# Norm weights as scales of the transposed copies instead of a spread row, and 24 identity transposes on TensorE before the first tile

## The chip, the cores and the metric

The kernel runs on one core of one Trainium2 chip. The metric is the device time of one execution in microseconds (us); lower is better.

## What is computed

One encoder layer is applied with the same weights to two requests: a prompt of 512 tokens and a sample of 1024 tokens, each 1024 wide, all in float32. Cut to what matters here:

```
h    = x * rsqrt(mean(x*x) + 1e-6) * g            # RMSNorm, g = norm_g (1024 weights)
proj = h @ w_in                                   # q, k, v of two attentions, gates z_a, z_b, g_a, g_b
oa   = neighbourhood attention(A) * silu(z_a);  ob = windowed attention with 8 heads on 2 k/v heads (B) * silu(z_b)
y    = x + (sigmoid(g_a) * (oa @ w_o_a) + sigmoid(g_b) * (ob @ w_o_b)) @ w_out
```

The norm weights g belong to the 1024 columns of x. The change concerns only the place where they are multiplied in for the prompt.

## The kernel before

**Precision.** Products are made of rounded parts: every operand v is kept as a high part (v rounded to the type fp32r) and a low part (v minus its high part), and each product is three matmuls, high by high, high by low, low by high. The parts of h are the tiles `hh` and `hl`, those of a weight piece `whi` and `wlo`. ScalarE (ACT) makes the high part with a copy, VectorE (DVE) or GpSimd (POOL) the low part with a subtraction.

**The order of the work.** The whole program is written as a list of operations with a priority, a guessed duration per engine and the operations that come before each (class `Flow`). A planner goes through them in a simulated time and lets each engine take the ready operation of the lowest priority number; where DVE and POOL can both do one, it picks the engine. What comes out is one fixed order of instructions per engine; on the chip the engines wait for each other by semaphores. So guessed durations set the order on every queue, also far behind the place where they stand. Operations that may run on either DVE or POOL, and those marked `port`, aren't planned on DVE and POOL at the same time. The piece `wlo` of the first weights is tied to POOL alone (`FIRST_POOL`), and an operation with one engine has no such mark unless it is given.

**The start.** The prompt is taken in four tiles t of 128 tokens. For each tile (`norm_tile`), with priority `NORM[t]` = -20, -1, 0, 1:

- SP's queue loads x into `xt`, 128 tokens on partitions by 1024 columns; ACT squares it and sums the squares (L460); POOL makes 1/rms per token, `nr`, in two steps (L464, L468).
- DVE multiplies `xt` in place by `nr` (one number per partition) and by the norm weights (L520), which here lie along the columns and so are needed as a row on all 128 partitions.
- TensorE (PE) transposes 128x128 pieces (L532) into PSUM, ACT copies them to `hh` (L537) and DVE subtracts to `hl` (L542): two pieces k at a time for tile 0, four at a time for tiles 1 to 3.
- Then the projection of the tile for the first attention group follows: 24 matmuls of 384 columns (L761), three for each of the eight pieces k of the contraction.

**The spread row.** The weights come twice from memory: as `gx` (128 partitions by 8, L1618), used much later for the sample, and as a row `norm_row` of 1024 numbers into the first partition of the tile `gb` (L1621; its tile is called `rb`). Four matmuls with a stationary row of ones (`one`) spread that row over 128 partitions into two PSUM banks (L1629, two records each). For tile 0, DVE reads the weights from those banks; ACT then copies the banks into `gb` (L1641), from which tiles 1 to 3 read them.

**`wake`** can issue pairs of transposes of the identity matrix into a PSUM bank that nobody reads. With `WAKE = 0` it issues none. The identity is made by POOL at the start.

The lines of the first group of weights (L600 loads, L602 `whi`, L607 `wlo`) run beside the first tiles. The first group's third and fourth piece lie in a tile that is called `bias` in the profile. The projections of the first group for four tiles, q and k (transposes L861, copies L882 and L896, subtractions L887 and L901), the attention, and later the large products of the gates and the output (L1284 to L1286) follow. L1010 and L1008 multiply attention weights by one number per partition, on DVE and POOL.

## Time and profile before

| | us |
|---|---|
| median of 3 runs (lowest, highest) | 1154.29 (1154.1, 1159.04) |
| time of the profiled execution | 1153.98 |
| its span, first to last instruction | 1152.2 |
| PE busy in the span | 1136.3 |
| DVE, ACT, POOL busy | 846.0, 663.3, 300.1 |

The profile is of one execution. Its time lies 0.3 us under the median of the runs shown, and its span 1.8 us under its own time. Busy is what the instruction records cover; the records of neighbouring instructions on one engine may overlap, so that the distance from start to start is shorter than the length of one record.

### The profile page before, as it was taken

Reading aid. Unit: us, or ns where it says so; the run is one execution under the profiler, and the core shown is the slowest. Engines: PE = TensorE matmul, PEld = TensorE weight load, DVE = VectorE, ACT = ScalarE, POOL = GpSimd, SP = SyncE. Lnnn points to the kernel's source line nnn. Section 1 sums busy time; section 2 is a strip of 40 time slices with the busy share of each in tenths; the row PEclk is TensorE's granted clock in tenths of the full one; section 3 lists DMA queues with packets and bytes.
Section 4 is the critical chain, followed back from the end, with each engine's and each line's share of the span. In section 5 each row is a group of like instructions: output and inputs, shape, how many; then the busy total and the mean of one; then the engine's idle time right before and its main releaser. Section 6 shows DMA issues by size and latency. Waiting matters only on the chain.

```text
span 1152.2 us, 18508 instructions
## 1 busy us (share of the span) xinstructions
PE 1136.3 (99%) x6139; PEld 984.3 (85%) x6139; DVE 846.0 (73%) x1963; ACT 663.3 (58%) x1489; POOL 300.1 (26%) x403
## 2 busy tenths in 40 slices
PE   8999999999999999999999999999999999999998
PEld 7899888888888899999998888888888888788887
DVE  6887777587775478887777788865887655497984
ACT  6777997554343357666679899955534334243320
POOL 4753433000020054353333324410121210032110
PEclk9999999999999999999999999999999999999999
DMA  7754534478786522121221113227666334574062
GB/s 267 258 160 143 171 95 119 119 240 260 244 274 209 164 71 67 24 73 34 65 67 48 49 29 83 71 59 250 197 167 199 111 110 158 198 230 127 28 223 87
DMA packets 124705, 159.86 MB, mean 139 GB/s; under 512 B 28297, under 2 KB 66961, under 8 KB 124610
## 3 DMA queue, kind: packets, MB, share of 16 engines
q1 hardware_dynamic: 124610, 158.69, 45.1%
q8 instruction: 48, 0.79, 0.3%
q14 instruction: 47, 0.39, 0.1%
HBM read 121.93 MB, written 41.44 MB: 142 GB/s over the span
## 4 chain that ended last, share of the span: by engine, by line
PE 88%; ACT 5%; DMA 3%; DVE 2%; issue 1%; POOL 1%; SPq 0%; ACTq 0%; POOLq 0%; DVEq 0%
PE p L761 21%; PE x L1285 9%; PE x L1286 9%; PE x L1284 9%; PE x L1063 5%; PE x L1026 4%; PE p L1284 4%; PE p L1285 4%; PE p L1286 4%; PE x L934 4%; PE d L1284 4%; PE d L1286 4%; PE d L1285 4%; ACT hb L662 2%; PE x L861 1%
## 5 line engine op out<-in xcount | busy, mean ns | idle before, releaser
L761 PE MATMUL p<-wlo,hh 128*128 128x384 f32 x384 | 133.3, 347 | 0.0
L761 PE MATMUL p<-whi,hh 128*128 128x384 f32 x384 | 133.0, 347 | 0.0
L761 PE MATMUL p<-whi,hl 128*128 128x384 f32 x384 | 131.8, 343 | 0.0
L978 ACT ACTIVATE sb<-sb,mx 128x384 f32<-128x384 f32 (+1 forms) x192 | 108.1, 568 | 16.5 <-DVE mx L969 16.3
L1167 ACT ACTIVATE whi<-raw 128x512 fp32r<-128x512 f32 (+1 forms) x140 | 81.3, 591 | 55.4 <-PE x L1285 32.2
L761 PE MATMUL p<-whi,hb 128*128 128x384 f32 x384 | 108.6, 347 | 1.6 <-ACT hb L662 1.5
L1037 DVE TENSOR_TENSOR pp<-x,pp 128x512 fp32r<-128x512 f32 (+1 forms) x136 | 83.1, 639 | 32.7 <-ACT pp L1032 31.9
L1285 PE MATMUL x<-hl,whi 128*128 128x512 f32 x264 | 102.7, 389 | 0.0
L1284 PE MATMUL x<-hh,whi 128*128 128x512 f32 x264 | 102.7, 389 | 0.0
L1286 PE MATMUL x<-hh,wlo 128*128 128x512 f32 x264 | 102.7, 389 | 0.0
L1172 DVE TENSOR_TENSOR wlo<-raw,whi 128x512 fp32r<-128x512 f32 (+1 forms) x113 | 72.0, 647 | 31.7 <-ACT whi L1167 31.7
L1284 PE MATMUL x<-T,whi 128*128 128x512 f32 x224 | 87.2, 390 | 1.5 <-ACT T L1167 1.5
L1285 PE MATMUL x<-T,whi 128*128 128x512 f32 x224 | 87.3, 390 | 0.2 <-DVE T L1172 0.2
L1286 PE MATMUL x<-T,wlo 128*128 128x512 f32 x224 | 87.1, 389 | 0.0
L1032 ACT ACTIVATE pp<-x 128x512 fp32r<-128x512 f32 (+1 forms) x136 | 72.1, 563 | 20.5 <-PE x L1026 19.7
L799 POOL TENSOR_TENSOR rs_r<-rs_v,mhalf 128x4 f32<-128x4 f32 (+1 forms) x72 | 80.5, 1119 | 5.3
L1172 POOL TENSOR_TENSOR wlo<-raw,whi 128x512 fp32r<-128x512 f32 x27 | 39.0, 1449 | 160.0 <-ACT whi L1167 113.7
L1063 PE MATMUL x<-pp,v 128*128 128x256 f32 (+1 forms) x368 | 78.8, 326 | 1.2 <-DVE pp L1037 1.2
L761 PEld LDWEIGHTS p<-whi,hb 128*128 128x128 f32 x384 | 69.2, 188 | 5.9 <-ACT hb L662 2.7
L761 PEld LDWEIGHTS p<-wlo,hh 128*128 128x128 f32 x384 | 72.8, 190 | 1.2 <-issue 0.5
L761 PEld LDWEIGHTS p<-whi,hl 128*128 128x128 f32 x384 | 72.7, 189 | 1.1 <-issue 1.0
L761 PEld LDWEIGHTS p<-whi,hh 128*128 128x128 f32 x384 | 72.7, 190 | 0.7 <-issue 0.5
(352 smaller groups left out, 2954.0 us busy)
## 6 DMA issues: line engine op xcount, KB each, us to landing
raw<-in_w_g_dram SPq DMA_DIRECT2D x76, 256.0 KB, 3.2
w<-in_w_att_dram SPq DMA_DIRECT2D x46, 384.0 KB, 3.5
ot<-o_d SPq DMA_DIRECT2D x36, 256.0 KB, 3.2
g_d<-C SPq DMA_DIRECT2D x34, 256.0 KB, 2.0
raw<-in_w_z_dram SPq DMA_DIRECT2D x32, 256.0 KB, 4.0
raw<-in_w_out_dram SPq DMA_DIRECT2D x32, 256.0 KB, 3.0
C<-g_d SPq DMA_DIRECT2D x24, 256.0 KB, 4.0
out_dram<-C SPq DMA_DIRECT2D x23, 256.0 KB, 2.0
```

Of the source, the lines that this page charges most:

```text
L761: pe.matmul(ps.t[:, :GW], part[u](k), mv.t[:, c], start=k == 0 and m == 0, stop=k == KC - 1 and m == 2,)
L799: lambda e: nc.gpsimd.tensor_tensor(r.t[:, :nn], rv.t[:, :nn], mhalf[:, :nn], op=ALU.pow),
L934: pe.matmul(pss[2 * pair + i].t[:, :width], q.t[rows, u, at : at + P], kv[:, tiles[0] : tiles[-1] + 1 : step], start=n == 0, stop=n == 2,)
L978: act.activation(sb.t[:, :width], sb.t[:, :width], AF.Exp, bias=mx.t[:, i : i + 1], scale=-1.0, accum_out=sm.t[:, i : i + 1],)
L1032: lambda e, pt=pt, pp=pp, nn=nn: act.activation(pp.t[:, 0, :nn], pt.t[:, :nn], AF.Copy),
L1037: lambda e, pt=pt, pp=pp, nn=nn: dve.tensor_tensor(pp.t[:, 1, :nn], pt.t[:, :nn], pp.t[:, 0, :nn].bitcast(F32), op=ALU.subtract),
L1063: pe.matmul(out(), v.t[:, vs], mv(), start=first, stop=last)
L1167: (("act", ACT_(n)),), lambda e: act.activation(hi(), src(), AF.Copy), prio,
L1172: lambda e: engines[e].tensor_tensor(lo(), src(), hi().bitcast(F32), op=ALU.subtract), prio,
L1284: pe.matmul(out, hi.t[:, cs], mh(), start=first and k == 0, stop=False)
L1285: pe.matmul(out, hi.t[:, cs], ml(), start=False, stop=False)
L1286: pe.matmul(out, lo.t[:, cs], mh(), start=False, stop=last and k == len(ws) - 1)
```

## The change

`norm_row`, its load, the ones, the four spreading matmuls and ACT's two copies of their banks go. DVE multiplies `xt` by `nr` alone, with a `tensor_scalar` whose operands all lie in SBUF. After the transpose the columns of x lie on partitions, so the weight is one number per partition: ACT's copy to `hh` takes it as its scale, and DVE's subtraction becomes a `scalar_tensor_tensor` that multiplies the transposed piece by the same number and subtracts `hh`. Each works on one piece k of 128 columns, since every piece has its own column of `gx`; so there are eight copies and eight subtractions per tile instead of four (tile 0) or two (tiles 1 to 3). The load of `gx` moves to the place of the row's load, second in SP's queue. `WAKE` becomes 12: 24 transposes of the identity, with priority 2 and nothing that they wait for but the identity.

```diff
-WAKE = 0
+WAKE = 12
@@ encoder_kernel
-    one = cpool.tile([1, P], F32, tag="one", name="one")
-    dve.memset(one, 1.0)
@@ norm_tile
-            ps, made = gains_row[k0 // 4]
-            if t == 0: ... weights from the PSUM bank ps
-            else: ... weights from gb.t, "port": True
             m = f.op(
-                (("dve", DVE_(n) + 60),),
-                lambda e, cols=cols, gv=gv: dve.scalar_tensor_tensor(
-                    xt.t[:, cols], xt.t[:, cols], r.t, gv(), op0=ALU.mult, op1=ALU.mult
-                ),
-                prio, **kw,
+                (("dve", 68 + 0.68 * n),),
+                lambda e, cols=cols: dve.tensor_scalar(xt.t[:, cols], xt.t[:, cols], r.t, None, op0=ALU.mult),
+                prio, use=[r], hold=[xt], port=True,
             )
...
-            a = f.op(
-                (("act", ACT_(n, False)),), lambda e, ks=ks, pv=pv: act.activation(hh.t[:, ks, tok], pv(), AF.Copy),
-                prio, use=[ps], hold=[hh],
-            )
-            b = f.op(
-                (("dve", DVE_(n)),),
-                lambda e, ks=ks, pv=pv: dve.tensor_tensor(
-                    hl.t[:, ks, tok], pv(), hh.t[:, ks, tok].bitcast(F32), op=ALU.subtract
-                ),
-                prio, use=[ps], after=[a], hold=[hh, hl],
-            )
-            out += [a, b]
+            for k in range(k0, k0 + step):
+                pv, gain = lambda k=k, ps=ps, k0=k0: ps.t[:, (k - k0) * P : (k - k0 + 1) * P], gx[:, k : k + 1]
+                to = lambda v, k=k: v.t[:, k, t * P : (t + 1) * P]
+                a = f.op(
+                    (("act", 250),), lambda e, pv=pv, gain=gain, to=to: act.activation(to(hh), pv(), AF.Copy, scale=gain),
+                    prio, use=[ps, gx_v], hold=[hh],
+                )
+                b = f.op(
+                    (("dve", 260),),
+                    lambda e, pv=pv, gain=gain, to=to: dve.scalar_tensor_tensor(
+                        to(hl), pv(), gain, to(hh).bitcast(F32), op0=ALU.mult, op1=ALU.subtract
+                    ),
+                    prio, use=[ps], after=[a], hold=[hh, hl],
+                )
+                out += [a, b]
@@ the start
-    f.dma(lambda: nc.sync.dma_start(gx, norm_g), 4096, 1, into=[gx_v])
+    f.dma(lambda: nc.sync.dma_start(gx, norm_g), 4096, START[0] + 0.1, into=[gx_v])
     wake()
-    gb = f.value(rb_pool, [P, NT_S], F32, "rb", 1)
-    row = f.dma(lambda: nc.sync.dma_start(gb.t[:1], norm_row.unsqueeze(0)), 4096, START[0] + 0.1, new=[gb])
-    gains_row = ... four matmuls with `one` into two banks
     for t in range(gp.nb):
         h_ops["p"][t] = norm_tile(
-            norm_p, x_p, gb, gains_row, *h_p, t, ...
+            norm_p, x_p, *h_p, t, ...
         )
-        for i, (ps, users) in enumerate(gains_row if t == 0 else ()):
-            ... ACT copies the bank into gb
```

## Rows read from the trace of the kernel before

**Rows 1.** The page: busy time of each engine, and PE's granted clock in 40 slices.

```profile
PE 1136.3 (99%) x6139; PEld 984.3 (85%) x6139; DVE 846.0 (73%) x1963; ACT 663.3 (58%) x1489; POOL 300.1 (26%) x403
...
PEclk9999999999999999999999999999999999999999
```

**Rows 2.** PE's waits after 10 us, longest first: total, times, longest.

```profile
PE x L1284 <- ACT T L1167: 1.5, 1, 1.5
```

**Rows 3.** PE's timeline from 4 to 17 us: start, length, instruction, count.

```profile
4.58 3.75 PE L1629 MATMUL x<-rb,one 1*128 1x256 f32 x8 [4.58 <-DMA rb<-in_norm_row_dram]
8.26 2.36 PE L532 MATMUL x<-ident,xt 128*128 128x128 f32 x8
10.27 0.67 PE L761 MATMUL p<-whi,hh 128*128 128x384 f32 x1
10.74 0.52 PE L761 MATMUL p<-wlo,hh 128*128 128x384 f32 x1
11.06 0.52 PE L761 MATMUL p<-whi,hl 128*128 128x384 f32 x1
...
13.55 0.34 PE L761 MATMUL p<-wlo,hh 128*128 128x384 f32 x1
...
14.24 0.34 PE L761 MATMUL p<-whi,hl 128*128 128x384 f32 x1
14.42 0.60 PE L532 MATMUL x<-ident,xt 128*128 128x128 f32 x4
...
16.72 0.34 PE L761 MATMUL p<-whi,hl 128*128 128x384 f32 x1
```

**Rows 4.** Timeline of the first 9 us, POOL and DVE.

```profile
0.99 0.29 POOL masks.py:199 TENSOR_SCALAR_AFFINE_SELECT ident<-ident 128x128 f32<-128x128 f32 x1
...
5.87 0.57 POOL L468 TENSOR_TENSOR nr<-nv,mhalf 128x1 f32<-128x1 f32 x1
6.40 1.81 POOL L607 TENSOR_TENSOR wlo<-w,whi 128x768 fp32r<-128x768 f32 x1
6.85 0.87 DVE L520 SCALAR_TENSOR_TENSOR xt<-xt,nr,x 128x256 f32<-128x256 f32 x2 [5.85 <-PE x L1629]
7.64 1.39 DVE L607 TENSOR_TENSOR wlo<-w,whi 128x768 fp32r<-128x768 f32 x1
```

**Rows 5.** Groups by line and shape, first 36 us: busy us, mean ns of one.

```profile
L542 DVE TENSOR_TENSOR hl<-x,hh 128x512 fp32r<-128x512 f32 x6 | 4.1, 690 | 2.3 <-ACT hh L537 2.2
L537 ACT ACTIVATE hh<-x 128x512 fp32r<-128x512 f32 x6 | 3.6, 598 | 5.1 <-PE x L532 5.1
...
L607 DVE TENSOR_TENSOR wlo<-bias,whi 128x768 fp32r<-128x768 f32 x2 | 1.9, 948 | 0.0
...
L882 ACT ACTIVATE kt<-x,gcol 128x128 fp32r<-128x128 f32 x3 | 1.1, 371 | 1.3 <-PE x L861 1.1
...
L887 DVE SCALAR_TENSOR_TENSOR kt<-x,gcol,kt 128x128 fp32r<-128x128 f32 x3 | 1.0, 350 | 1.5 <-ACT qt L896 1.5
```

**Rows 6.** Timeline around 448 and 460 us, DVE and POOL.

```profile
448.30 0.75 DVE L1010 TENSOR_SCALAR sb<-sb,rs 128x384 f32<-128x384 f32 x2
...
460.82 1.11 DVE L1010 TENSOR_SCALAR sb<-sb,rs 128x384 f32<-128x384 f32 x2
...
460.00 1.71 POOL L695 TENSOR_TENSOR bias<-mask,raw 128x192 f32<-128x192 f32 x3 [0.77 <-DVE mx L969]
```

**Rows 7.** Instructions on tile `xt`: ns min/median/max, first to last start, forms.

```profile
L532 PE MATMUL x<-ident,xt x32: 271/273/476, 8.3 to 28.5; 128*128 128x128 f32 x32
```

**Rows 8.** ACT's timeline from 15 to 22 us; idle time before in brackets.

```profile
15.06 0.60 ACT L537 ACTIVATE hh<-x 128x512 fp32r<-128x512 f32 x1 [2.24 <-PE x L532]
...
21.15 0.37 ACT L882 ACTIVATE kt<-x,gcol 128x128 fp32r<-128x128 f32 x1 [1.15 <-PE x L861]
21.42 0.36 ACT L896 ACTIVATE qt<-x,gq 128x128 fp32r<-128x128 f32 x1
```

**Rows 9.** Timeline of SP's queue at the load of `gx`.

```profile
4.79 0.43 SPq L1618 DMA_DIRECT2D gx<-in_norm_g_dram  x1
```

More of the change, by code (lines that the diff above doesn't have):

```diff
@@ L362, in encoder_kernel @@
     norm_g: bass.AP,
-    norm_row: bass.AP,
     w_att: bass.AP,
@@ L503, in scaled_parts, with norm_tile @@
         return out
-    def norm_tile(pool, x, gb, gains_row, hh, hl, t, prio, load_prio, after=(), load_after=()):
+    def norm_tile(pool, x, hh, hl, t, prio, load_prio, after=(), load_after=()):
         xt, r = rstd(pool, x, t, prio, load_prio, 4, after, load_after)
-        tok = slice(t * P, (t + 1) * P)
         step, out = 2 if t == 0 else 4, []
         for k0 in range(0, KC, step):
-            n, cols, ks = step * P, slice(k0 * P, (k0 + step) * P), slice(k0, k0 + step)
-            ps, made = gains_row[k0 // 4]
-            if t == 0:
-                c = slice(k0 % 4 * P, k0 % 4 * P + n)
-                gv, kw = lambda ps=ps, c=c: ps.t[:, c], {"use": [r], "hold": [xt, ps], "after": [made[k0 % 4 // 2]]}
-            else:
-                gv, kw = lambda cols=cols: gb.t[:, cols], {"use": [r], "hold": [xt, gb], "after": made, "port": True}
-            m = f.op(
-                (("dve", DVE_(n) + 60),),
-                lambda e, cols=cols, gv=gv: dve.scalar_tensor_tensor(
-                    xt.t[:, cols], xt.t[:, cols], r.t, gv(), op0=ALU.mult, op1=ALU.mult
-                ),
-                prio, **kw,
-            )
-            if t == 0:
-                made.append(m)
+            n, cols = step * P, slice(k0 * P, (k0 + step) * P)
+            m = f.op(
+                (("dve", 68 + 0.68 * n),),
+                lambda e, cols=cols: dve.tensor_scalar(xt.t[:, cols], xt.t[:, cols], r.t, None, op0=ALU.mult),
+                prio, use=[r], hold=[xt], port=True,
+            )
             ps = bank("x")
@@ L1617, in encoder_kernel @@
     f.stage(-1000, open=(r_h, d0["p"], rb_pool, early["p"], late["p"], norm_p), make=h_p)
-    f.dma(lambda: nc.sync.dma_start(gx, norm_g), 4096, 1, into=[gx_v])
+    f.dma(lambda: nc.sync.dma_start(gx, norm_g), 4096, START[0] + 0.1, into=[gx_v])
     wake()
-    gb = f.value(rb_pool, [P, NT_S], F32, "rb", 1)
-    row = f.dma(lambda: nc.sync.dma_start(gb.t[:1], norm_row.unsqueeze(0)), 4096, START[0] + 0.1, new=[gb])
-    gains_row = []
-    for i in range(2):
-        ps, made = bank("x"), []
-        for j in range(2):
-            cols, out = slice(i * 512 + j * 256, i * 512 + j * 256 + 256), slice(j * 256, j * 256 + 256)
-            made.append(f.op(
-                (("pe", 850),),
-                lambda e, ps=ps, cols=cols, out=out: pe.matmul(ps.t[:, out], one, gb.t[:1, cols], start=True, stop=True),
-                NORM[0] - 1, hold=[gb], after=[row], **({"into": [ps]} if j else {"new": [ps]}),
-            ))
-        gains_row.append([ps, made])
     for t in range(gp.nb):
         h_ops["p"][t] = norm_tile(
-            norm_p, x_p, gb, gains_row, *h_p, t, NORM[t], START[t], h_ops["p"][t - GATE][::2] if t >= GATE else (),
+            norm_p, x_p, *h_p, t, NORM[t], START[t], h_ops["p"][t - GATE][::2] if t >= GATE else (),
             h_ops["p"][0][-1:] if t > 1 else (),
         )
-        for i, (ps, users) in enumerate(gains_row if t == 0 else ()):
-            gains_row[i][1] = [f.op(
-                (("act", ACT_(512, False)),),
-                lambda e, ps=ps, i=i: act.activation(gb.t[:, i * 512 : i * 512 + 512], ps.t, AF.Copy),
-                NORM[1] - 1, use=[ps], hold=[gb], after=users[2:],
-            )]
     setup(norm_p, -0.7, h_ops["p"][1][:1])
@@ L1728, in _layout @@
         "norm_g": inp["norm_g"][0].reshape(KC, P).T,
-        "norm_row": inp["norm_g"][0],
         "w_att": np.stack(groups),
```

1 line of the change is left out of this document (removed).

## The prediction

> **What bounds the kernel now.** I read the page first. PE is busy for 1136.3 of 1152.2 us and the granted clock is at its upper level, 2.4 GHz, in every slice [rows 1]. The list of PE's waits comes next: after 10 us the longest single one is 1.5 us [rows 2]. So from about 10 us on the kernel is one nearly unbroken stream of matmuls. Its end is the time at which that stream starts, plus the PE work, plus few small gaps. The change touches only the first 30 us, so I went on to PE's timeline there.
>
> PE first spreads the weight row, from 4.58 to 8.33 us; then it transposes tile 0; the first projection matmul starts at 10.27 us and the last of tile 0, the 24th, ends at 16.72 + 0.34 = 17.06 us [rows 3]. The distance from start to start is the thing to look at: 11.06 - 10.74 = 0.32 us early on, but (14.24 - 13.55) / 4 = 0.173 us later, for the same 384 columns [rows 3]. 384 columns in 0.32 us is 1.2 GHz. The slices of the page don't show this start, the pace does. Ten matmuls take 13.55 - 10.27 = 3.28 us, at the later pace 1.73: the low clock costs 1.55 us here. Before it rose PE had been at the spreading matmuls for 3.75 us (a stationary operand of one row), at eight transposes and at three microseconds of full matmuls.
>
> Then the timeline of the other engines, to see what tile 0 waits for. `nr` is ready at 5.87 + 0.57 = 6.44 us; DVE's first multiplication starts at 6.85 and is put down to PE's spread; a `wlo` of 1.39 us stands between DVE's second and third [rows 4].
>
> **The change, part by part.** The sum is made against the profiled execution's 1153.98 us, 0.3 us under the median of the runs.
>
> *The row goes.* Two waits end: DVE's for the spread (6.85 instead of about 6.5) and that of PE, which couldn't transpose before 8.26. DVE loses one memset in idle time, the PSUM banks of the row are free earlier. ACT's two copies of 128x512 go, about 0.6 each by the like-shaped copies [rows 5].
>
> *What DVE's multiplication meets instead.* It becomes an operation whose operands are all in SBUF. POOL starts its `wlo` of 1.81 us at 6.40, a moment before DVE could start, and holds on until 8.21 [rows 4]. Do the two get in each other's way? Three rows bear on it. The old multiplication with weights in PSUM took 0.87 for two beside this same POOL instruction. DVE's `wlo`, all in SBUF, started at 7.64 in its second half and took 1.39, where the same shape takes 0.948 elsewhere [rows 4, 5]: 0.44 longer, as if it stood until 8.08. And two `tensor_scalar` of 128x384 took 0.75 at one place and 1.11 beside POOL subtractions [rows 6]. I take it that DVE's first multiplication stands until 8.08. The other bound is a start at 6.5. The planner doesn't see this: `wlo` of the first piece is tied to POOL and carries no mark.
> The Trainium skill says the same more sharply (SBUF — State Buffer, section "SBUF: two separate sides"): DVE and GpSimd share one pair of ports, which goes as an exclusive lock for a whole instruction to whichever starts first, and a DVE operation wants it with two SBUF inputs or in a two-port mode. By that rule the multiplication stands until 8.21; without it the first projection would start some 1.6 us sooner.
>
> *From there to the first projection matmul.* One `tensor_scalar` of 128x384 costs 0.34 to 0.41 from the pair in 0.75 [rows 6], and 128x256 is no longer: 8.08 + 0.37 = 8.45. A transpose's record is 0.273 long in the middle of its group, and four took 0.60, so they start (0.60 - 0.273) / 3 = 0.11 apart at the high clock and, taken twice, 0.22 at the low one [rows 3, 7]. Two of them, with the length of the second and the hand-overs, end at 8.9 to 9.0. One copy with a scale per partition costs 0.371 [rows 5]: 9.3 to 9.4. I put the first matmul at 9.4, against 10.27.
>
> *Then the supply of the 24.* PE itself needs 24 x 0.173 = 4.15 us and two fours of tile 1's transposes at up to 0.60 [rows 3]: 9.4 + 4.15 + 1.2 = 14.75 at the high clock, 1.55 more, 16.3, at the low one. DVE from 8.08 has four multiplications (4 x 0.3 = 1.2), eight subtractions of 0.27 to 0.350 (the longer end is the row's record, the shorter is the distance that ACT's like pair shows, 21.42 - 21.15 [rows 5, 8]; 2.2 to 2.8), three `wlo` of 0.948 (2.85) and two multiplications of tile 1 (about 0.45 each): it ends at 15.2 to 15.8, and its last pieces may lie behind tile 0's end. I take 15.2 for the end of tile 0 against 17.06: 1.86 us.
>
> *The 24 transposes of the identity.* The identity is ready at 0.99 + 0.29 = 1.28 [rows 4]. At 0.22 us each they end at 1.4 + 24 x 0.22 = 6.7, ahead of the 8.45 at which PE is next wanted, so they cost nothing. At the pace of tile 0's eight with their pauses, 2.36 / 8 = 0.30 each [rows 3], they end at 8.6. Whether they raise the clock no row shows. The spread's one-row matmuls kept PE at work for 3.75 us and the clock stayed low after them; but these transposes fill 128 by 128, like the matmuls under which it rose. I take it that they raise it. DVE being the limit, this is worth not 1.55 but 16.3 - 15.2 = 1.1 at most.
>
> *Tiles 1 to 3.* ACT makes 24 copies, started every 0.27, instead of six of 0.598: 6.5 - 3.6 = 2.9 us more. Its idle time before two instructions of this stretch alone is 2.24 + 1.15 = 3.39 [rows 5, 8], and PE can begin on a single piece. DVE makes 24 subtractions (6.5 to 8.4) instead of six of 0.690 (4.1), and saves some 2 us on its six multiplications of 512 columns (two of 256 took 0.87 [rows 4], the new ones about 0.45). If ACT's idle time can't be used the 2.9 are PE's; I charge 0.1. Lower bound nothing, upper 2.9.
>
> *The load of `gx`.* It goes from the tenth place of SP's queue to the second; its issue of 0.43 us [rows 9] now stands ahead of the first weights and tile 1's x, in place of the row's issue, and leaves a gap in front of tiles 2 and 3. That is a shift of 0.1 to 0.2 for loads that nothing waits on by that much; nothing, up to 0.4.
>
> Sum: 1.86 - 0.1 = 1.8 us gained, 1153.98 - 1.8 = 1152.2. PE's stream behind it is the same and carries this to the end.
>
> **Rivals.**
>
> *The clock stays low.* Then tile 0 ends at 16.3 instead of 15.2, and the gain is 17.06 - 16.3 = 0.8, less 0.1: 1153.3. For it speaks that 3.75 us of PE work on the spread didn't raise the clock; against it that those were one row wide.
> The Trainium skill has this as a rule (TensorE: Matmul & The Clock Gate, section "PE-mode transpose"): the full clock doesn't engage for transposes, since they don't count as PE activity in the same way. No row here has transposes alone for long, so the trace neither bears it out nor refutes it.
>
> *DVE isn't held by POOL.* The chain starts 1.6 us sooner, first matmul at 7.8, DVE's supply ends at about 14; with POOL's `wlo` at 8.21 still wanted by the second matmul, tile 0 ends at 14.2 to 14.8. Gain 2.3 to 2.9: 1151.4.
>
> *The gain is given back.* ACT's idle gaps lie where it waits for transposes, so the 2.9 more may not fit into them; two thirds of it on PE's path eat the gain: 1154.0, within 1 us to either side.
>
> *Slower: the identity transposes hold PE.* If at the low clock they aren't pipelined, 24 records of the longest length, 0.476 [rows 7], end at 1.4 + 11.5 = 12.9 instead of 8.45; the first matmul is then at 13.8, tile 0 ends at 19.2, and the kernel takes 1156.2. It decides from (8.45 + 1.86 - 1.4) / 24 = 0.37 us each. Against it: eight transposes at the low clock took 2.36 us with pauses among them [rows 3].
>
> *The rest of the plan falls out differently.* New guesses and fewer operations shift every later decision between DVE and POOL. PE's idle time after 10 us is small, the longest piece 1.5 [rows 2], so little is to be won there: some 4 us more by a lucky order would bring 1148. A transfer that comes too late can cost more, with four or five waits of that size 1160.
>
> **Numbers.** Forecast 0.28; clock stays low 0.18; DVE not held 0.15; given back 0.12; PE held by the identity 0.05; another order 0.22 (0.10 ends over 0.5% faster, 0.07 over 0.5% slower, 0.05 between). 0.5% is 5.8 us, about what a measurement of this kernel tells from no change. Every case but the last two parts of another order lies inside that: 0.10 faster, 0.83 same, 0.07 slower. The forecast is 1152.2, its own range 1151 to 1153.5 from 15.8 and 14.75 for tile 0's end and the bounds of tiles 1 to 3 halfway. The range for 8 in 10 takes in the rivals up to the held PE and a part of the other orders: 1147.5 to 1156.2.
>
> **What would show it.** The first projection matmul starts near 9.4 and tile 0's last ends near 15.2. DVE's first `tensor_scalar` has a record of nearly 2 us or starts near 8.1; at 6.5 with 0.4 the port step is wrong. The first projection matmuls are 0.17 apart if the clock is up, 0.32 if not. Of PE's identity transposes the last ends before 7. ACT's idle brackets between 13 and 28 us shrink, and PE gets no new wait for `hh`. The prediction fails if PE's stream shows other gaps after 40 us than before: that would be the order, not the start.

## The result, and the profile after

The changed kernel takes 1157.91 us (median of 20 runs, 1156.18 to 1162.68) against 1154.34 us of before (20 runs, 1152.53 to 1159.04). The ratio is 1.0036 with a 95% interval of 1.0025 to 1.0046: slower, by less than the 0.5% that the prediction called no change, but outside its range of 1147.5 to 1156.2. The profiled execution took 1157.09 us, with a span of 1155.3. Three runs of the experiments that follow, one of f_order and two of f_dve0, took 1250 us or more and are left out of every figure.

The page of the changed kernel answers to [rows 1]. TensorE is as full as before; nothing here says where 3 us went.

```profile
PE 1140.2 (99%) x6155; PEld 986.1 (85%) x6155; DVE 844.8 (73%) x1971; ACT 664.8 (58%) x1507; POOL 303.2 (26%) x418
...
PEclk9999999999999999999999999999999999999999
```

PE's timeline of the first 18 us answers to [rows 3].

```profile
1.34 5.36 PE L442 MATMUL d<-ident 128*128 128x128 f32 x24 [1.34 <-POOL ident masks.py:199]
6.94 0.44 PE L518 MATMUL x<-ident,xt 128*128 128x128 f32 x2 [0.23 <-DVE xt L510]
8.76 0.96 PE L518 MATMUL x<-ident,xt 128*128 128x128 f32 x6 [1.37 <-DVE xt L510]
9.47 0.42 PE L749 MATMUL p<-whi,hh 128*128 128x384 f32 x1
9.73 0.34 PE L749 MATMUL p<-wlo,hh 128*128 128x384 f32 x1
10.41 0.69 PE L749 MATMUL p<-whi,hl 128*128 128x384 f32 x1 [0.34 <-DVE hl L530]
10.89 0.52 PE L749 MATMUL p<-whi,hh 128*128 128x384 f32 x1
11.21 0.52 PE L749 MATMUL p<-wlo,hh 128*128 128x384 f32 x1
...
15.52 0.34 PE L749 MATMUL p<-whi,hl 128*128 128x384 f32 x1
15.69 1.03 PE L518 MATMUL x<-ident,xt 128*128 128x128 f32 x8
17.78 0.44 PE L749 MATMUL p<-whi,hh 128*128 128x384 f32 x1 [1.06 <-ACT hh L525]
```

The identity transposes end at 6.70 and the first projection matmul starts at 9.47 (it was 10.27). What stood in between isn't quite what was forecast. VectorE's first scaling took 0.35 us, as GpSimd's `wlo` started only 0.12 us behind it; it was the second that stood (the two together read `6.53 2.17`). ScalarE had a new wait of 1.09 us for the second weights, so that its first copy came at 8.42. VectorE and GpSimd at the first scaling, then ScalarE:

```profile
6.53 0.35 DVE L510 TENSOR_SCALAR xt<-xt,nr 128x256 f32<-128x256 f32 x1 [5.67 <-POOL nr L465]
6.65 1.89 POOL L595 TENSOR_TENSOR wlo<-w,whi 128x768 fp32r<-128x768 f32 x1 [0.16 <-ACT whi L590]
```

```profile
7.67 0.84 ACT L590 ACTIVATE whi<-w 128x768 fp32r<-128x768 f32 x1 [1.09 <-DMA w<-in_w_att_dram]
```

On to the clock. The first two projection matmuls are 0.34 to 0.42 long, the next ones 0.52 and 0.32 apart: the clock was up and fell again. The windows of the same trace say when (start:end, length, busy time and count of each engine, granted clock, DMA share, GB/s); the clock is at 0.50, its lower level, from about 10 to 13.3.

```profile
6.50:10.00 3.50, 1.89 (x12) 1.08 (x10) 3.47 (x5) 2.20 (x8) 1.89 (x1) 1.00 0.99 382
10.00:13.30 3.30, 2.96 (x10) 2.89 (x10) 3.30 (x11) 3.30 (x8) 0.00 (x0) 0.50 1.02 406
13.30:17.00 3.70, 3.42 (x23) 3.15 (x21) 2.18 (x6) 1.20 (x4) 1.24 (x3) 0.99 0.70 228
```

Tile 0's 24th matmul ends at 15.86 in place of 17.06. But the eight transposes of tile 1, which before stood among the 24, now stand behind them and end at 15.69 + 1.03 = 16.72: for the same work the lead is 0.34 us. Then tile 1 loses it. PE waits 1.06 us for the copies, and ScalarE's timeline shows why: it squares tile 2 first, from 16.32 on, and makes the eight copies from 17.36. This is read from the trace; no run moved the square. TensorE's matmul at 17.78 follows the end of the first copy, 17.36 + 0.37, so it doesn't wait for the others.

```profile
16.32 1.06 ACT L457 ACTIVATE junk<-xt 128x1024 bf16<-128x1024 f32 x1
17.27 0.20 ACT L457 ACTIVATION_READ_ACCUMULATOR junk<-xt 128x1 f32 x1
17.36 2.17 ACT L525 ACTIVATE hh<-x,gx 128x128 fp32r<-128x128 f32 x8
```

PE's waits after 10 us answer to [rows 2]. The wait of 1.5 us of before is gone, others are there:

```profile
PE x L849 <- DVE qk L804: 1.3, 3, 0.8
PE p L749 <- ACT hh L525: 1.1, 1, 1.1
...
PE x L1272 <- ACT hh L1155: 0.9, 1, 0.9
```

To place them I laid the two streams of matmuls over each other: each matmul counts with its time at the full pace for its columns, and the table gives, for a moment of the profiled run of before, how much later (in us) the other kernel's profiled run had done as much work. It is my working from the traces, of all the kernels that follow too. Each row is one execution, which can lie off its kernel's median: f_wake38's took 1155.47 us (median 1158.18), b_wake's 1158.30 (1156.18), a_guess1's 1170.06 (1167.45).

```
time in before    12    19    27    37    62   163   310   365   431   527   970  1002
after           -0.5   1.6   1.3   1.6   1.4   1.9   2.5   4.1   3.5   4.6   4.5   3.2
a_nowake        -0.3   1.5   1.2   1.5   1.5   2.3   2.9   7.7   7.2   7.2   6.9   6.3
a_guess1        -0.1   4.0   3.8   4.5   4.4   9.6  10.0  17.0  16.6  18.1  17.9  16.0
a_ot3           -0.5   1.8   1.5   1.7   1.4   2.7   3.3   4.4   3.9   4.9   4.9   3.5
f_order          0.3  -0.1   1.6   1.8   2.1   2.4   2.4   2.4   2.4   2.4   2.3   2.1
f_wake38        -0.7  -1.0   0.6   0.8   1.1   0.9   0.9   0.9   1.2   2.2   2.0   1.2
f_gx5            0.2  -0.1   1.5   1.7   2.5   1.8   1.8   1.8   1.2   2.6   2.5   1.1
f_dve0          -0.4   0.6   2.2   2.4   2.3   1.7   1.7   2.1   1.5   1.5   1.4   0.8
f_nowake         0.3   0.5   2.1   2.3   2.7   2.3   2.3   2.3   1.9   1.9   1.9   0.6
f_fill          -0.7  -0.8   0.8   1.0   1.3   1.3   1.2   1.4   2.5   3.3   3.2   2.2
f_nosplit        1.1   2.1   1.9   1.5   2.8   2.6   2.7   2.7   2.0   3.3   3.1   2.4
f_fill_ns       -0.7  -1.3  -1.6  -2.0  -0.9  -1.4  -1.4   0.3   1.3   2.4   2.2   0.8
b_wake           1.7   1.2   1.2   1.2   2.4   3.2   3.2   3.2   4.5   5.5   5.2   4.3
b_guess1         0.4   0.5   0.3  -0.1   1.5   1.2   2.1   2.1   1.9   1.9   1.8   1.3
b_lag1950       -0.3  -1.0  -0.6  -0.6   0.5  -2.2  -2.2  -2.2  -3.3  -3.1  -4.6  -6.4
a_lag1950       -0.4   0.5   0.2  -0.1   2.0  -0.7  -0.7  -0.7  -1.7  -1.5  -2.8  -5.1
b_lag2950        0.2   0.6   3.5   3.4   3.0   1.7   3.5   3.5   2.5   2.2   2.1  -0.3
a_lag2950       -0.3   1.5   1.2   1.2   0.5  -0.6   0.4   0.4  -0.6  -0.9  -1.1  -3.4
```

The changed kernel is ahead at 12 us, 1.6 behind at 19, and 1.4 at 62: the start, the whole of what the change edits, costs 1.4, and it is lost between 16.7 and 19 us. Another 1.1 comes bit by bit from 62 to 310, and then it is single places: 1.6 at 361 (the wait of 0.9 for `hh` above, and what follows it), 1.1 at 523 (a wait of 0.8 for `qk`, the longest of the three above). Some 0.6 comes back before 431 and 1.3 near 985, where before had its wait of 1.5 us [rows 2] and this kernel has none.

No instruction out there was edited. But the planner writes out the order of all engines from guessed durations, and it made another order: of the 6131 matmuls that both traces have, the spread and the identity transposes apart, at least 324 stand at another place. So there are two theories: A, the order far behind the start costs the time; B, the change's own instructions cost it.

### The profile page after: what moved, and what is told of

Its sections match the earlier page's. It is cut to its first block, busy times and chain, and to the rows that moved or that the text cites. A ratio compares the mean times of both kernels' runs of the same rounds, so it can differ in the third digit from the quotient of the medians.

```text
span 1155.3 us, 18585 instructions
## 1 busy us (share of the span) xinstructions
PE 1140.2 (99%) x6155; PEld 986.1 (85%) x6155; DVE 844.8 (73%) x1971; ACT 664.8 (58%) x1507; POOL 303.2 (26%) x418
## 4 chain that ended last, share of the span: by engine, by line
PE 81%; ACT 7%; DMA 4%; DVE 4%; issue 2%; POOL 1%; SPq 0%; ACTq 0%; DVEq 0%; POOLq 0%
PE p L749 21%; PE x L1273 9%; PE x L1274 8%; PE x L1272 8%; PE x L1051 4%; PE x L1014 4%; PE x L922 4%; PE p L1273 4%; PE p L1272 4%; PE p L1274 4%; PE d L1272 3%; PE d L1273 3%; PE d L1274 3%; ACT hb L650 2%; PE x L849 1%
## 5 line engine op out<-in xcount | busy, mean ns | idle before, releaser
L966 ACT ACTIVATE sb<-sb,mx 128x384 f32<-128x384 f32 (+1 forms) x192 | 108.7, 573 | 17.2 <-DVE mx L957 16.9
```

Source lines behind the costliest of these rows:

```text
L966: act.activation(sb.t[:, :width], sb.t[:, :width], AF.Exp, bias=mx.t[:, i : i + 1], scale=-1.0, accum_out=sm.t[:, i : i + 1],)
```

## The experiments

Kernels f_ have the change's instructions in the order of before: the planner is given before's operations and durations, and only what they emit is the change's. One thing is not as in the change: an operation of before covers a whole bank, so a kernel f_ issues a bank's copies one after the other and its subtractions behind them, where the change plans each piece by itself. Kernels a_ are the change itself, b_ the kernel before, each with the edit shown. Each experiment had runs of before beside it, with medians of 1153.36 to 1153.85; all ratios are against those.

**The order and the instructions apart.**

```
f_order:  planner's operations and durations as before;
          what they emit as in the change (24 transposes where the row was spread)
b_guess1: -                (("dve", DVE_(n) + 60),),
          +                (("dve", 68 + 0.68 * n),),
a_nowake: -WAKE = 12
          +WAKE = 0
f_wake38: f_order with 38 identity transposes in place of 24
```

f_order: 

> The change's instructions (multiplication by 1/rms alone, copies and subtractions with the weight as scale, 24 identity transposes, early load of the weights, no spread row) in the order of the kernel before on every engine: the planner is given the operations of before with their guesses. Theory A, that the other order behind the start costs the time: as fast as before or faster, 1152 to 1154.5 us. Theory B, that the change's own instructions cost it (more ACT and DVE work, DVE held by POOL, a clock that falls back): 1157 to 1159 us, like the changed kernel.

b_guess1: 

> The kernel before with every instruction as it was; only the planner's guess for the multiplication at the start is the one of the change, 68 + 0.68 n instead of 128 + 1.04 n ns. That moves about as many instructions in the queues as the change did. Theory A: it is off from before by 1 us or more, in either direction, with a gap or two of PE that before doesn't have. Theory B: within 0.7 us of before, 1153.6 to 1155.

a_nowake: 

> The changed kernel without the 24 identity transposes; every other instruction stands in the same order on every engine. If the transposes raise the clock and it is lost again before the projections: within 0.5 us of the changed kernel, 1157.4 to 1158.4, with the projections 0.32 us apart until about 13.4 in both. If the transposes delay the start: faster by 0.5 to 1 us. If the high clock at the first pieces is worth something: slower by 0.3 to 0.6 us.

f_wake38: 

> As the run with the order of before, but 38 identity transposes instead of 24, which at the high clock last until about 8.2 us and so leave no pause of PE before the first tile's transposes. If the clock of the changed kernel fell because PE stood between 6.7 and 9.5 us, the projections start at the high clock and stay there, tile 0 ends up to 1.5 us sooner than with 24, and the time is 0.5 to 1.5 us below that run. If the transposes don't hold the clock up, 0.32 us apart from about 10 to 13.4 as with 24, and no difference.

Measured: f_order 1155.93 us, ratio 1.0022 (1.0013 to 1.0032); b_guess1 1154.53, 1.0006 (0.9997 to 1.0015); a_nowake 1159.28, 1.0047 (1.0035 to 1.0060); f_wake38 1158.18, 1.0040 (1.0025 to 1.0054). Neither theory is alone right. In the order of before the change still costs 2 us, between 19 and 37 us in the table, and has no stall at 361: between what A and B had forecast. One guess changed in before moves its stream by up to 2.1 us on the way, and its median hardly, as B had it. The identity transposes are worth nothing that the total shows: a_nowake lies at 1.0047, its interval overlapping the change's, and f_nowake, further down, takes what f_order takes. They do raise the clock; without them, in the same order, the first two projection matmuls are at the lower pace:

```profile
9.97 0.67 PE L749 MATMUL p<-whi,hh 128*128 128x384 f32 x1
10.44 0.52 PE L749 MATMUL p<-wlo,hh 128*128 128x384 f32 x1
```

But there the records are short from 13.00 on, in the change only from 13.43 on. In f_wake38, where TensorE stood for 0.63 us behind the identity transposes and not for 1.93 as in f_order, the clock stays up and the start is 1 us sooner. The windows of f_order and of f_wake38:

```profile
10.00:13.30 3.30, 3.30 (x13) 3.30 (x14) 2.97 (x10) 3.30 (x10) 0.68 (x2) 0.55 1.02 408
10.00:13.30 3.30, 3.15 (x19) 2.77 (x20) 3.30 (x11) 2.99 (x8) 0.51 (x1) 1.00 1.04 421
```

Its median is higher than f_order's all the same, where 0.5 to 1.5 us less was expected; its profiled run is its shortest and doesn't show why.

a_nowake's trace shows what a stall can draw after it. PE's waits of 355 to 372 us:

```profile
PE x L1272 <- ACT hh L1155: 2.3, 1, 2.3
```

and its windows behind that wait; the clock is at its lower level for 3.4 us, so that the stall cost it 4.8 us in all (2.9 to 7.7 in the table):

```profile
360.00:364.60 4.60, 2.09 (x9) 1.10 (x7) 3.21 (x7) 2.41 (x5) 1.28 (x1) 1.00 0.61 179
364.60:368.00 3.40, 3.40 (x8) 2.38 (x8) 2.50 (x4) 1.04 (x2) 0.00 (x0) 0.50 0.86 277
```

**The 2 us that stay in the order of before.** In f_order the first copies and subtractions of tile 2 read so, ScalarE's timeline and VectorE's:

```profile
22.89 1.14 ACT L535 ACTIVATE hh<-x,gx 128x128 fp32r<-128x128 f32 x4
```

```profile
24.06 1.12 DVE L540 SCALAR_TENSOR_TENSOR hl<-x,gx,hh 128x128 fp32r<-128x128 f32 x4 [0.94 <-ACT hh L535]
```

VectorE waits until all four copies of the bank are made, and then needs 1.12 us. Before it was one copy of 0.598 and one subtraction of 0.690 [rows 5]. In the changed kernel itself VectorE doesn't wait so: in tile 3 its first subtraction starts at 25.29, while the third copy lasts until 24.64 + 0.88 = 25.52, and in the table that kernel loses nothing between 19 and 62 us. So what f_order loses can't be carried over to the change as the cost of its pieces.

```profile
24.64 0.88 ACT L525 ACTIVATE hh<-x,gx 128x128 fp32r<-128x128 f32 x3 [0.49 <-PE x L518]
```

```profile
25.29 0.33 DVE L530 SCALAR_TENSOR_TENSOR hl<-x,gx,hh 128x128 fp32r<-128x128 f32 x1
```

Three edits to f_order take one suspect each; f_nosplit takes the pieces away:

```
f_nosplit: f_order, ScalarE's copy and VectorE's subtraction whole for each bank, no weights
f_gx5:     f_order, load of gx issued behind w0, w1 and xt of tile 1, not second
f_dve0:    f_order, +  e = "dve" if engs == ("pool",) else e      (the first wlo)
a_guess1:  the change, planned durations only: copy 250 -> 371, subtraction 260 -> 350
```

f_nosplit: 

> f_order (the change's instructions in the order of before) with the copies and subtractions whole again, as before: one ScalarE copy and one VectorE subtraction for each bank in place of four of each; the norm weights are left out of the prompt altogether, so the output lacks them there. Theory B1, that the 48 split pieces cost f_order its time (a bank's subtraction starts 1.14 us after its first copy in place of 0.60 and takes 1.13 in place of 0.69, for six banks behind tile 0): tiles 2 and 3 end about 1 us sooner than in f_order, and the time is 1153.5 to 1154.5, at most that of before. Theory B2, that the early load and the held VectorE cost it: the time stays at about 1156 (ratio to before 1.002).

f_gx5: 

> f_order with one edit: the 128-packet load of the norm weights is issued fifth on SyncE's queue, behind w0, w1, xt0 and xt1, instead of second. Theory B2 (the packets of 32 bytes keep the 16 DMA engines from the large loads in the first 6 us): ScalarE's second whi of w1 waits under 0.2 us where it waited about 1.1, the DMA rate of 3 to 6 us goes back from 354 to about 410 GB/s, and the time is 0.5 to 1 us lower than f_order's (about 1155.2). Theory B1 (the split pieces cost it): the start looks like that and the time stays at about 1156. If the load now comes too late for tile 0's first copy, that copy starts later than in f_order by the lateness.

f_dve0: 

> f_order with one edit: the first wlo subtraction, which GpSimd does from 6.6 to 8.1 us while VectorE's first scaling of tile 0 is held, is done by VectorE behind that scaling. Theory of the prediction (the scaling is held by GpSimd's work): the first scaling takes about 0.4 us in place of 2.1, tile 0's transposes end about 1 us sooner (8.8 in place of 9.8), and the first projection matmul comes at about 9.6 to 10 in place of 10.6; the time falls by at most that 1 us and, if the lead is lost again behind the start as in f_wake38, by nothing (1156). Rival: the scaling waits for its data; then it stays at 2 us and nothing moves.

a_guess1: 

> The change with every instruction as it is, and only the two planned durations by which its order is made put to what the trace shows for the split pieces (ScalarE's copy planned at 371 in place of 250 ns, VectorE's subtraction at 350 in place of 260). Theory A (the order far behind the start decides a few us): the progress of TensorE departs from the change's by 1 to 3 us at places far behind the start, such as the stall at 361, and the time differs from the change's by 1 us or more either way. Theory B (the change's own instructions): the time stays within 1 us of the change's 1157.9.

Measured: f_nosplit 1155.67, 1.0018 (1.0006 to 1.0031); f_gx5 1154.70, 1.0015 (1.0005 to 1.0025); f_dve0 1155.02, 1.0017 (1.0007 to 1.0027); a_guess1 1167.45, 1.0128 (1.0098 to 1.0159). The first three can't be told from f_order by their time, so what they say is read from the traces.

f_gx5: the DMA rate of 3 to 6 us is 408 GB/s, against 354 in f_order, 326 in the changed kernel and 410 in before, and ScalarE's wait of 1.0 for the second `w` is gone. Over all profiles it is less clear. With the load second in the queue (11 kernels) the rate is 322 to 370 and that wait 0.6 to 2.2 us; with it fifth (f_gx5, f_fill, f_fill_ns, f_fill_ot3) 374 to 408 and none to 0.3. But before and the four b_ kernels, without it at the start, have 348 to 410 and none to 0.8. So the load holds back the large ones, but single executions of before differ by nearly as much. At 12 us TensorE has 0.1 us of it.

f_dve0's first scaling shows that GpSimd had held it; in f_order its two took `6.51 2.15`:

```profile
6.44 0.35 DVE L518 TENSOR_SCALAR xt<-xt,nr 128x256 f32<-128x256 f32 x1 [5.58 <-POOL nr L466]
6.71 0.95 DVE L606 TENSOR_TENSOR wlo<-w,whi 128x768 fp32r<-128x768 f32 x1
```

The first projection matmul then comes at 9.90 in place of 10.61; the low clock lasts to 15.2 us, and the lead is used up.

f_nosplit has no wait of PE at all from 17 to 34 us, where f_order has 2.1, but its start is 0.8 us later (ScalarE waited 2.2 us for the second weights, and the second `wlo` is at 9.37 in place of 8.58) and its clock stays low until 16.8, which eats the 2 us: not decided by its time, which lies where the theory B2 had it.

a_guess1 is the large one: every instruction as in the change, two planned durations put to what the trace shows, and the time rises by 0.9%. Its table row loses at 19, between 62 and 163, and 7 us at 361. The order alone moves this kernel by 9.5 us. A good part of that goes through the clock. Where TensorE had stood (for 1.73 us until 163.73, for 2.33 until 372.49), it fell again:

```profile
163.70:167.10 3.40, 3.37 (x14) 3.33 (x15) 3.08 (x10) 2.38 (x6) 0.20 (x1) 0.50 0.24 67
371.90:378.70 6.80, 6.21 (x14) 4.67 (x15) 2.58 (x4) 1.68 (x3) 0.00 (x0) 0.50 0.67 229
```

With 10.1 to 16.9 us that is 17.0 us at the lower level against 3.4 in the changed kernel. The same matmul takes about twice as long there (0.32 against 0.173 from start to start), so my estimate is half of the 13.6 us between them, 6 to 7 of the 13.0 us between the two profiled runs.

**The start mended, and each half alone.**

```
b_wake:    before, -WAKE = 0   +WAKE = 12       (order of all the rest unchanged)
f_nowake:  f_order without the identity transposes
f_fill:    f_gx5 and f_dve0 together, and ahead of tile 0's later transposes
           +  for u in range(6 if t == 0 and k0 else 0):
           +      pe.transpose(ps.t[:, u % 2 * P : u % 2 * P + P], ident, ident)
f_fill_ns: f_fill with whole copies and subtractions, no weights
```

b_wake: 

> The kernel before with the 12 pairs of identity transposes alone; all other instructions and their order are those of before. Theory: the 24 transposes end at about 6.5 to 6.7 us, the rows of the spread matmuls behind them run at the higher clock (under 2 us in place of 3.4 us), and tile 0's transposes then wait for its squares and scaling as before. If the clock stays up, tile 0's last matmul ends 1 to 2 us sooner than 17.06; if it falls again at about 10 as in the change's trace, under 1 us. The total moves by at most that, 1152.5 to 1154 against 1153.5 of before; with the lead lost behind the start it is the same. The prediction's rival that identity transposes only hold TensorE would give up to 0.3 us more than before.

f_nowake: 

> f_order without the identity transposes: the norm weights as scales alone, in the order of before. Theory B1 (split copies and subtractions cost about 2 us in tiles 1 to 3, the head gives some of it back): first matmul at about 10 to 10.6 at the lower clock until about 13.4, tile 0 ends at 16.5 to 17, the gaps of 20 to 31 us stay at about 3.4 us in all against 1.05 in before, and the time is 1.5 to 2.5 us above before (1155 to 1156). Rival: the transposes themselves cost it; then it is at 1153.5 to 1154.5.

f_fill: 

> f_order with the load of the norm weights fifth on the queue, the first wlo subtraction on VectorE, and 6 more identity transposes ahead of each of tile 0's second, third and fourth group of transposes, so that TensorE hardly stands between 6.5 and 9.5 us. Theory (the granted clock fell to 0.50 for 3.4 us behind the first matmuls because TensorE had mostly stood between the identity transposes and them): the clock now stays at 1.0, tile 0's 24 projection products come 0.17 apart, and its last ends at 14 to 15 us in place of 17.06 of before. Then 2 to 2.5 us are lost to the split copies of tiles 1 to 3, and the time is 1153 to 1154.5, about that of before. Rival: the fall comes at fixed times and not from standing; then the low stretch stays.

f_fill_ns: 

> f_fill with whole copies and subtractions, one for each bank, as before; the norm weights are left out of the prompt, so the output lacks them there. Theory B1 (the split pieces lose about 2 us in tiles 1 to 3): the gaps of 17 to 32 us fall from about 3.4 us to about 1, the lead of tile 0 is kept, and the time is 1 to 2 us lower than f_fill's, below that of before (1151.5 to 1152.5). Theory A2 (any lead at the start is lost behind it at the weights and loads that pace the rest): the time is within 0.5 us of f_fill's though the gaps are gone.

Measured: b_wake 1156.18, 1.0024 (1.0011 to 1.0038); f_nowake 1155.52, 1.0018 (1.0005 to 1.0030); f_fill 1155.88, 1.0016 (1.0004 to 1.0028); f_fill_ns 1154.27, 1.0003 (0.9992 to 1.0014).

b_wake, which I had expected at or below before, starts its first projection matmul at 11.98 in place of 10.27: with the spread's matmuls still there the transposes hold TensorE, the last six of them among tile 0's own. Alone, the wake costs 1.2 us at the start. The 18 transposes ahead of the spread (4.10 us) didn't raise the clock here: the spread takes 3.78 us where it took 3.75, under 2 being expected, and the first projection matmuls are 0.32 apart.

f_fill keeps the clock up. Its windows, to be held against those of the changed kernel above (PE busy for 2.89 in place of 1.89 us, then 1.00 in place of 0.50):

```profile
6.50:10.00 3.50, 2.89 (x22) 2.42 (x23) 2.88 (x6) 2.19 (x5) 0.27 (x2) 1.00 1.02 379
10.00:13.30 3.30, 3.01 (x20) 2.69 (x19) 3.11 (x10) 3.17 (x9) 0.57 (x1) 1.00 1.03 417
```

So the clock had fallen behind TensorE's standing, which f_wake38 against f_order shows with that edit alone; no fixed time does it. Tile 0's 24 and two fours of transposes end at 15.91 + 0.34 = 16.25, not at the 14 to 15 expected: the first comes at 10.36 only, and two fours of transposes, a gap of 0.46 us with a wait for `wlo`, lie between. And f_fill loses 1.6 us between 19 and 27, f_fill_ns doesn't. PE's waits of 17 to 34 us in f_fill, where f_fill_ns has none:

```profile
PE x L867 <- DVE qk L822: 1.2, 2, 0.8
PE x L535 <- DVE xt L523: 0.9, 2, 0.7
```

That settles it for this order and for pieces issued bank by bank: they cost 2.1 us of waits in tiles 1 to 3. (The two intervals of the total overlap; the waits are what decides.) But f_fill_ns, 2.0 us ahead at 37, ends 0.8 behind: it loses 1.7 at 361, 1.0 at 400, 1.1 at 521, the same places where the changed kernel and others lose, each at some of them.

**What stands at those places.** f_gx5 and f_dve0 have the same order there, and one stalls at 521 and the other doesn't. VectorE's timeline in f_gx5:

```profile
520.81 1.59 DVE L698 TENSOR_TENSOR bias<-mask,raw 128x192 f32<-128x192 f32 x4 [1.18 <-DMA raw<-rpb_x]
522.33 0.41 DVE L819 TENSOR_TENSOR qk<-p,rs_r 128x256 f32<-128x256 f32 x1
```

and in f_dve0:

```profile
519.96 1.03 DVE L694 TENSOR_TENSOR bias<-mask,raw 128x192 f32<-128x192 f32 x4
520.78 0.97 POOL L694 TENSOR_TENSOR bias<-mask,raw 128x128 f32<-128x128 f32 x2
520.92 0.41 DVE L815 TENSOR_TENSOR qk<-p,rs_r 128x256 f32<-128x256 f32 x1
```

The load into `raw` was issued at 516.75 in f_gx5 and used from 520.8 on; in f_dve0 at 517.04, and used from 519.96 on. Where it lands late, `qk` stands behind `bias` in VectorE's order, and PE waits 1.26 us for `qk`. The changed kernel's stall at 523 reads the same, `522.73 1.58` with 0.75 of wait for the same load. At 361 it is ScalarE's `hh` that PE wants; it stands 2.11 us for VectorE's `C`, at the end of a chain of such copies and sums in which ScalarE waits 6.3 us for `ot<-g_d` loads between 338 and 365 (before: 5.1, with no stall).

**A third buffer, and a plan with slack.**

```
a_ot3, f_fill_ot3: -n_c, n_ot = (4, 2) if short else ...
                   +n_c, n_ot = (4, 3) if short else ...
a_lag1950, b_lag1950, a_lag2950, b_lag2950 (planner: when a load counts as landed):
                   -at(dma_free + 950, 2, got)
                   +at(dma_free + 1950, 2, got)      (2950)
```

a_ot3: 

> The change with three in place of two ot buffers in the prompt's part (the space is that of the row of ones that the change removed); TensorE's order is the same, SyncE's differs in 83 lines. Theory (the merge before 361 us is paced by loads into two ot buffers, each issued when a merge step frees one): the loads ot<-g_d are issued a step sooner, ScalarE's waits on them fall from 6.3 us in 338 to 365 us to under 2, the last hh<-C comes before 359 and TensorE's stall of 1.6 us at 361 to 363 is gone. The time falls by 1.5 us or more (to 1156 or lower), and its runs scatter less. Rival (the lag is made up elsewhere or shows up as another stall): the stall goes and the time stays at 1157 to 1158.

f_fill_ot3: 

> f_fill with three ot buffers. f_fill has no stall at 361 in its profiled run, so that by the theory of a_ot3 little changes there: 0 to 0.5 us less than f_fill's 1155.9. If orders with the same TensorE work differ by a us or more through such a step, that is the scatter of single late loads.

a_lag1950: 

> The change with an order planned for loads that land 1 us later than it assumed before; the instructions are the same, about a thousand of TensorE's rows stand elsewhere. Theory (far stalls come from loads that land later than planned while work that TensorE needs stands behind the instruction that waits for them): the stalls at 361, 404 to 410 and 521 become rarer, and the time falls to 1153 to 1156. Rival: buffers and not issue times set when loads start, so the plan moves other things about and the time is anywhere within 1155 to 1165.

b_lag1950: 

> The kernel before with an order planned for loads that land 1 us later. By the theory of a_lag1950 it stays within 1 us of 1153.9 or falls below; by the rival it is 1 to 10 us above. Together with a_lag1950 it gives the change's effect under a second pair of orders, which differ from each other in 56 of TensorE's rows: if the change's own instructions cost 2 us, a_lag1950 is about 2 us above b_lag1950.

a_lag2950: 

> The change with an order planned for loads that land 2 us later than first assumed. Theory (the order decides, the change's own effect is under 1 us): within 1 us of b_lag2950, or off it by a few us either way for stalls that stand behind 34 us in the trace. Theory (own cost of 2 us or more): 1.5 to 4 us above b_lag2950, with the difference in the trace before 36 us. Both lie between 1147 and 1153 if more slack goes on helping.

b_lag2950: 

> The kernel before with an order planned for loads that land 2 us later: 1147 to 1152 if more slack goes on helping, above 1150.5 if it now starts transfers that other loads wait behind.

Measured: a_ot3 1156.18, 1.0020 (1.0009 to 1.0031); f_fill_ot3 1155.78, 1.0020 (1.0009 to 1.0031); a_lag1950 1149.38, 0.9968 (0.9957 to 0.9980); b_lag1950 1150.47, 0.9975 (0.9966 to 0.9984); a_lag2950 1151.60, 0.9986 (0.9977 to 0.9994); b_lag2950 1155.02, 1.0010 (1.0000 to 1.0020).

a_ot3 is mostly a miss. ScalarE's waits for `ot` in 338 to 365 us fall from 6.3 to 5.6 and not under 2, and the stall at 361 goes from 1.6 to 1.1. The buffers alone don't pace those loads. The time is lower by 0.16% with overlapping intervals, and the runs scatter less (1154.09 to 1157.67), so that something may have been gained, though not where it was expected. f_fill_ot3 takes what f_fill takes, as expected.

The orders planned for loads 1 us later are faster, the change's by more than the 1153 to 1156 expected. With the same instructions, the change in the order for loads 1 us later is at 0.9968 where it was at 1.0036, and its 7 runs lie between 1148.59 and 1150.90, where the 20 of the change lay between 1156.18 and 1162.68. PE's longest waits after 10 us in a_lag1950; those for `hh` at 361 and for 0.8 at 523 are gone:

```profile
PE x L1051 <- DVE pp L1025: 1.2, 3, 0.7
PE x L849 <- DVE qk L804: 0.8, 2, 0.6
```

The gain isn't these two alone: in the table a_lag1950 goes from 2.0 behind at 62 to 0.7 ahead at 163, and gains again between 527 and 1002. It is the fastest kernel measured, 0.32% below before. b_lag2950 shows that more slack isn't always more: it loses 3 us between 19 and 27, where TensorE waits 1.41 us for `xt` and the granted clock is then at 0.50 from 24.7 to 28.1. Whether it is the slack that helps, or an order that happens to be better, these four orders don't tell.

Under three pairs of orders, then, the change against its counterpart stands at +3.6 per mille (1.0036), at -0.7 (0.9968 against 0.9975, intervals overlapping) and at -2.4 (0.9986 against 1.0010, apart). In the order of before it is +2.2, and in the order of a_guess1 +12.8 against before in its own.

## Why the prediction was wrong

*The first projection matmul.* Right in the number, 9.47 against 9.4, and in part by luck. That GpSimd holds VectorE's scaling is right, and f_dve0 shows it (0.35 without it). But here GpSimd came second: the first scaling took 0.35, which the prediction had named as the sign of a wrong step, and the second stood for 1.9 us, until 8.70. The Trainium skill's rule on this (SBUF — State Buffer, "SBUF: two separate sides") agrees with the trace, where GpSimd's `wlo` ended at 8.54. And TensorE was at the other six transposes until the first matmul, so that ScalarE's copy, the last link of the forecast, wasn't what it waited for.

*The identity transposes.* They ended at 6.70 as worked out and raised the clock: the matmuls at 9.47 and 9.73 ran at the upper level, those of a_nowake at the lower. The Trainium skill's sentence that the full clock doesn't engage for transposes (TensorE: Matmul & The Clock Gate, "PE-mode transpose") differs from this trace; the measurement decides. But the step assumed that a raised clock stays. TensorE stood for 1.6 of the 2.8 us between 6.70 and 9.47, and the clock fell for the next 3.4 us; f_fill, which fills that time, keeps it.

*Tile 0's end.* 16.72 for the work that was put at 15.2: 0.34 of the 1.86 us. From the first matmul it is 7.25 us, where 5.8 was put down. With the clock up it is 5.89 in f_fill and 5.75 in f_wake38, in the order of before, so most of the difference is the clock's; whether the supply was sized right for the change's own order was not tried. The rival "the clock stays low", with 16.3, was nearer. (Both of the prediction's bounds for TensorE are some 0.5 high: its 0.60 for four transposes is the length of their records, and in before the next matmul starts 0.36 behind them, at 14.78.)

*Tiles 1 to 3.* Charged 0.1 with bounds 0 and 2.9. In the change's order, from 0.34 ahead to 1.6 behind is 1.9 us, all of it at tile 1. That PE can begin on a single piece was right there (17.78, behind the first copy). What failed is that ScalarE's idle gaps can be used: it stood for 2.50 us until 15.89, because tile 1's transposes had moved behind tile 0's 24 matmuls, and then squared tile 2 while the copies were wanted. Behind 19 us the pieces cost nothing more. In the order of before, bank by bank, they cost 2.1 us of waits for `qk` and `xt` (f_fill against f_fill_ns), where the change's own trace has 0.2 between 19 and 62 us. The rival "given back" had the size, two thirds of 2.9, and of the mechanism the gaps that don't fit, but not the order that made them.

*The load of `gx`.* Shifts of 0.1 to 0.2 were expected; ScalarE had a wait of 1.09 us for the second weights, only a part of which the load made. On TensorE's path f_gx5 shows 0.1.

*The steps that failed*, then, by the profiled run's 4.9 us above the forecast: at 62 us the kernel is 1.4 behind where the sum had it 1.8 ahead, 1.5 of these 3.2 us in tile 0's end (a raised clock taken to stay) and the rest in tiles 1 to 3 (charged 0.1). The other 1.7 is the sum's last step, "PE's stream behind it is the same and carries this to the end", put at nothing. The stream was another one: gaps between 62 and 310, the stalls at 361 and 523, and a stall of before near 985 that is missing, none of which any edit touches. The prediction had named gaps after 40 us as its sign of failing by the order. The rival "another order" was this, but I gave it 0.22 and bounded its gain at some 4 us by PE's longest waits. The runs put orders of the change's own instructions between 1149.4 and 1167.5 us. Reading that the waits are small, I took the order for settled; small waits may as well mean that many loads land just in time, and each can go either way.

*What stays open.* Whether the change has an effect of its own across orders: three pairs give both signs, and the 2 us in the order of before hold for pieces issued bank by bank. Which load will land late in a given run was seen, not predicted, and what sets off the stall at 361 was not found (a_ot3). Why the orders planned with slack gain between 62 and 163 and behind 970 was not taken apart.

## What to carry to other kernels

Where a planner writes out the order, a changed operation is a new order everywhere: its scatter has to be measured (a changed guess, the same instructions in the old order) before a few microseconds are put down to the edit. Where the profile shows loads that land later than the plan assumes, try the plan with more slack too: 1 us of it brought 0.25% below before without the change and 0.32% with it, 2 us brought 0.14% with the change and cost 0.10% without. And work split into pieces gains by that only where each piece is planned by itself: issued bank by bank, the subtractions waited for all four copies.

## What the runs showed of the hardware that I had not expected

TensorE's clock, once raised by 24 transposes of an identity, fell to 0.50 for about 3.4 us after TensorE had stood for 1.6 of 2.8 us (0.23 and 1.37 in its timeline), and the same happened at 364.6 us in a_nowake behind a single wait of 2.3 us; the stall of 0.85 and 0.22 us at 361 in the changed kernel left it at 1.0. The time of a run goes with it: of the changed kernel's 20 runs, those with a mean granted clock of 0.995 or 0.996 took 1161.19 to 1162.68 us, those with 0.999 or 1.000 all but one (1160.79) 1158.47 or less. One load of 128 small packets (4 KB in all), moved from second to fifth place in the queue (f_order to f_gx5), took the DMA rate of 3 to 6 us from 354 to 408 GB/s; five profiles without it there had 348 to 410.
